# A hybrid encoder block on one core: 252 intermediate stores move from SyncE's DMA queue to GpSimd's, and none of them is held back any more

## The chip, the core and the metric

The kernel runs on one core of one Trainium2 chip. A core has a matrix engine (TensorE, PE in the profile; its weight loads are listed as PEld), three engines for elementwise work (VectorE or DVE, ScalarE or ACT, GpSimd or POOL) and SyncE (SP), which in this kernel only issues DMA transfers. ScalarE and GpSimd issue DMA transfers too, so there are three queues: "SPq", "ACTq" and "POOLq" in the profile. An engine issues in the order of its program: an instruction that waits for a semaphore holds everything behind it on that engine.

The metric is the time on the device in microseconds (us), as the median of several executions. One further execution is taken with the hardware profiler; "the profile" and "the trace" mean that one.

## The reference, cut to what matters

The block works on x of 2048 frames by 1024 channels in float32, one layer deep.

```python
h = rmsnorm(x, norm_mix_pre)
u_pool, u_glu, g_a, g_b = split(h @ w_in)          # 512 | 1024 | 1024 | 1024 columns
# branch A: per group of 128 channels the trailing mean over 2, 4, 8 or 16 frames
#           minus the frame itself, a 128x128 map, a scale, then @ w_pool_out (512 -> 1024)
# branch B: a * sigmoid(gate), causal depthwise convolution of width 31 over 512 channels,
#           LayerNorm over the channels, silu, then @ w_conv_out (512 -> 1024)
merged = sigmoid(g_a) * branch_a + sigmoid(g_b) * branch_b
x = x + rmsnorm(merged @ w_o, norm_mix_post)
h = rmsnorm(x, norm_mlp_pre)
f = square(relu(h @ w_up)) @ w_down                # 1024 -> 4096 -> 1024
out = x + rmsnorm(f, norm_mlp_post)
```

## The kernel before, in words

*Layout.* Channels lie on the 128 partitions and frames run along the free axis. The 2048 frames are two blocks (b = 0, 1) of TB = 1024, each of two halves (t = 0, 1) of T = 512. The usual tile is 128 x 1024 in float32, 512 KB: a cell (256 channels by 512 frames), or a part of a weight.

*Matrix products.* Each float32 operand is split into a high part, rounded by a ScalarE copy (L225 for weights), and a low part, source minus high part, by a VectorE subtraction (`sub`, L121). `matmuls` (L268) adds three products: high by high, high by low, low by high. One call is 12 matmuls of 128 x 128 by 128 x 512 for four blocks of the contraction in the full form of `product`, which calls it for both halves of the output: 24 matmuls.

*Seven products for eight.* The class `Octet` computes a 2 x 2 scheme of cells by weight parts with seven block products, so weights and cells are needed not only as they are but as sums and differences. `weight_parts` makes those of a weight: `get` loads a raw part into one of four `wr` buffers, `minus` makes a sum in one of two `ws` buffers, `split_w` writes the high part into one of three `wh` buffers and the low part into one of three `wl` buffers. For block b = 0 the parts that will be needed again are stored in DRAM (`save`; the names are kept<-wl for low parts and kept<-ws for sums). For b = 1 they are loaded instead of made (wl<-kept, and the sums into `wr`). `load_w` does the same for the weights of the branches and of the output projection, `Plain` for the first part of the input projection.

*Stages.* TensorE's order is: input projection of b = 0 (glu, pool, gates ga and gb), branch A of b = 0, input projection of b = 1, branch B and merge of b = 0, output projection of b = 0, branch A of b = 1 (about 800 us), up projection of the MLP for b = 0, then branch B, merge and output projection of b = 1, the up projection for b = 1, and the down projection of both blocks until the end (the last 600 us), in which VectorE and ScalarE also form the cells of each step (`token_cells`). The final norm and the output stores come last. Convolution (L937), LayerNorm and pooling run on VectorE behind the products, spread over them by "lanes" that release a few steps after each product; those of b = 0 run while TensorE is at the input projection of b = 1.

*What passes through DRAM.* SBUF doesn't hold all intermediates, so these go to DRAM and come back: GLU results (vd, two halves per result) and pool inputs (ud), convolution and LayerNorm results (yd, stored from `y` after the convolution and from `tr` after the mean is taken off), results after the activation (zd) and after the pool map (mxd), sigmoids of the gates (sad, sbd), results of branch A (mad), x after the mixer (x1d), MLP activations and their sums (fd), sums of the down weights (wsum). The buffers from which they are stored (`tr` has 9, `big` 28, `y` one, `fo` five) come free when the store has landed.

*Queues.* Three helpers issue transfers: `load` on SyncE (L127), `aside` on GpSimd (L131) and `store` on ScalarE (L135). Despite its name, `load` carries all loads from DRAM but eight (x for the first output projection comes by `aside`) and most stores. `aside` also has the stores of the halos at the start, the first four low parts of `Plain`, and x1d of the first output projection. `store` has sad, sbd and the plain fd results. The final output goes by `load`, but two cells of it that GpSimd adds onto the output (L1878).

*The deferring lists.* Stores of kept weight parts are not issued where the part is made. `save` and `load_w` append them to the list `later`. After each product `flush` is called: it issues what is in `due` by `load`, last entry first, and moves `later` into `due`. So a part made before one product is issued as a store only after the next call.

*What sets the order.* The program is traced in the order of the Python code, and a planner then orders each engine's instructions by priorities: a region under `tc.high_priority(offset=n)` counts as n places earlier (260 for weights, `AHEAD`; 1500 for `URGENT`), and `mark`, `ordered` and `behind` add order without waiting. Instructions for one engine, DMA issues among them, come in one sequence. The planner also decides which buffer of a pool a tile takes.

Of the kernel before, what the change touches and what calls it, by code (L numbers as in the profile page):

```python
# [67 lines left out]
def block_kernel(  # L68
# [165 lines left out]
    def load_w(src, key):  # L234
        with tc.high_priority(offset=ahead[0]):
            raw = mk(p_wr, "wr")
            load(raw, src)
            known = kept.get((key, "low"))
            w = split_w(raw) if known is None else None
            if key is None:  # L240
                return w
        if w is None:
            with tc.high_priority(offset=260):
                w = split_w(raw, low=known)
        if known is None:
            kept[key, "low"] = dram("kept")
            later.append((kept[key, "low"], f32(w[1])))
        return w

    kept, later, due = {}, [], []  # L250

    def flush():

        while due:
            load(*due.pop())
        due.extend(later)
        later.clear()

# [46 lines left out]
    def weight_parts(src, key, b, keep, raw):  # L305
# [34 lines left out]
        def save(i, what, tile):  # L340
            kept[key, i, what] = dram("kept")
            later.append((kept[key, i, what], f32(tile)))

# [82 lines left out]
    class Octet:  # L426
# [18 lines left out]
        def run(self, i, then, bg):  # L445
            w, cells = self.w.pop(i, None) or self.weight(i), self.parts.need(i)
            if then is not None:
                self.parts.need(then)
            acc = {1: "x", 2: "z", 6: "x", 5: "y", 7: "x", 3: "y", 4: "x"}[i]
            if i in (1, 2, 5):  # L450
                self.ps[acc] = psum(self.lab)
            ps = self.ps[acc]
            product(ps, w, cells, start=i in (1, 2, 5), stop=i in (2, 3, 4))
            flush()
            if i == 1:
                self.s1 = self.held(ps)
                if self.s2 is not None:
                    self.sink(0, 0, self.s2, self.s1)
            elif i == 2 and self.s1 is None:
                self.s2 = self.held(ps)  # L460
            elif i == 2:
                self.sink(0, 0, ps, self.s1)
            elif i == 6:
                self.s6 = self.held(ps)
            elif i == 5:
                self.s5 = self.held(ps)
            elif i == 7:
                self.sink(1, 1, ps, self.s5)
            elif i == 3:
                self.sink(0, 1, ps, self.s6)  # L470
            else:
                self.sink(1, 0, ps, None)
            bg()
# [3 lines left out]
    class Plain:  # L477
# [30 lines left out]
        def run(self, job, then, bg):  # L508
# [7 lines left out]
            product(self.ps, w, cells, start=k == 0, stop=k == 1)  # L516
            flush()
            bg()
# [346 lines left out]
    def glu(b, parts):  # L865
        def one(u):
            sg = {}

            def sink(m, t, ps, s):
# [6 lines left out]
                if t in sg and (t, 1) in sg:  # L876
                    o = sg[t]
                    mul(o, o, sg[t, 1])
                    for i in (0, 1):
                        at = TAPS - 1 + b * TB + t * T  # L880
                        load(vd[2 * u + i][:, at : at + T], o[:, i * T : (i + 1) * T])

# [6 lines left out]
    def pool_in(b, parts):  # L889
        def sink(m, t, ps, s):  # L890
            o = block_out(ps, s)
            if o is ps:
                o = tr()
                mark(nc.scalar.copy(o, ps))
            for i in (0, 1):
                at = HALO + b * TB + t * T
                load(ud[2 * m + i][:, at : at + T], o[:, i * T : (i + 1) * T])

# [16 lines left out]
    def conv_steps(b, groups, ahead=True):  # L915
# [8 lines left out]
        for c in groups:  # L924
# [22 lines left out]
            else:  # L947
                add(sums[b], sums[b], acc)
            load(yd[b, c, 0], acc)
            yield  # L950

    def norm_steps(b, lag):
# [21 lines left out]
        for c in range(CC):  # L974
            if c + 2 < CC:
                prefetch(c + 2)
            sub(y[c], y[c], mu)
            load(yd[b, c, 0], y[c])
            sq = ss if c == 0 else tr()
# [16 lines left out]
        for c in range(CC + 1):  # L996
# [11 lines left out]
            if c:  # L1008
                mul(y[c - 1], y[c - 1], sg[c - 1])
                load(zd[b, c - 1, 0], y[c - 1])  # L1010
            yield 1
# [9 lines left out]
    def pool_steps(b, alone):  # L1021
# [9 lines left out]
        for g in range(CC):  # L1031
# [29 lines left out]
            yield  # L1061
            load(mxd[b, g, 0], o)
            yield
# [34 lines left out]
    def branch_a(b, mixed, bg):  # L1098
# [8 lines left out]
        for (c, t), sg in ahead_by_one(keys, gate_of, 2):  # L1107
# [5 lines left out]
            mark(i)  # L1113
            flush()
            with tc.high_priority(offset=URGENT):
                mark(mul(sg, ps, sg))
            load(mad[b, c, t], sg)
            bg()

    def merge(b, bg, made=none):  # L1120
# [11 lines left out]
        for (c, t), (sg, ma) in ahead_by_one(keys, gate_of, 1 + b):  # L1132
# [5 lines left out]
            mark(i)  # L1138
            flush()
            mark(mul(sg, ps, sg))  # L1140
# [12 lines left out]
    def out_proj(b, merged, halves, bg, made, early=none):  # L1153
# [13 lines left out]
        for ts in halves:  # L1167
            sq = {t: Squares(TR) for t in ts}
            for c in range(CPS):
                ws = [load_w(w_o[c % 2, 2 * (c // 2) + i], ("wo", c, i)) for i in (0, 1)]  # L1170
                for t in ts:
# [8 lines left out]
                    mark(i_mm)  # L1180
                    flush()
                    o[c, t] = mk(*BIG)
# [108 lines left out]
    def out_proj_2(b, cells, made):  # L1291
# [6 lines left out]
        def make(c, t):  # L1298
            mul(two(o[c, t]), two(o[c, t]), per_token(rbs[t]))
            add(x[c, t], x[c, t], o[c, t])  # L1300
            load(x1d[b, c, t], x[c, t])
            gained(o[c, t], x[c, t], C_MPRE, c)
# [35 lines left out]
        for n, (u, i) in enumerate(WO):  # L1338
# [6 lines left out]
            product(p, w, ops, start=i in (1, 2, 5), stop=i in (2, 4, 3))  # L1345
            flush()
            if i in (1, 6, 7):
# [50 lines left out]
    def mlp_up(b, parts):  # L1398
        def one(u):
# [3 lines left out]
            def sink(m, t, ps, s):  # L1403
# [7 lines left out]

                def keep(i, cell, how=load):
                    fd[b, u, i] = dram("fd")
# [254 lines left out]
    def weight_down(i, s, o):  # L1668
# [6 lines left out]
        def joined(op, p, q):  # L1675
            t = mk(p_ws, "ws")
            op(t, get(p), get(q))
            if i in (5, 6):
                wsum[s, o] = dram("wsum")
                load(wsum[s, o], t)  # L1680
            return t
# [12 lines left out]
    def token_cells(s, i, b, home=TR, hi_home=BIG):  # L1694
# [11 lines left out]
        with tc.high_priority(offset=AHEAD):  # L1706
            cells = []
            for j in (0, 1):
# [4 lines left out]
                if m is not None:  # L1713
# [4 lines left out]
                    if i == 6:  # L1718
# [3 lines left out]
                        fd[b, u, "t4"] = dram("fd")  # L1722
                        load(fd[b, u, "t4"], t4)
                hi = mk(*hi_home, F32R)
# [292 lines left out]
```

## Time and profile before

| | us |
|---|---|
| median of 3 runs | 2190.27 |
| lowest and highest | 2186.27, 2196.49 |
| the profiled execution | 2191.51 |
| its span (first to last instruction) | 2189.7 |
| TensorE busy | 2159.9 (99%) |
| VectorE busy | 1610.3 (74%) |
| ScalarE busy | 1017.6 (46%) |
| GpSimd busy | 18.2 (1%) |

The mean granted clock of TensorE in the profiled execution is 0.995 of full speed. In all, 552.30 MB are moved.

How to read the rows: `L121 DVE` is line 121 of the kernel on VectorE; `wl<-kept` is an operation that writes a tile named wl from one named kept (for a DMA, the transfer from DRAM to the buffer); `x72` is a count. A row of waits names the engine that waited, what it wanted to run, and after the arrow what ended the wait, with total us, number of waits and the longest. A row of the chain gives start, length and what ran; the chain is followed back from the last instruction, to what released each step. In the list of DMA issues, the three numbers with slashes are the shortest, median and longest time in ns that an issue takes on its engine.

### The profile page before, as it was taken

The numbers are of one execution on the slowest core, as the hardware profiler recorded it, in microseconds if no ns is written. First come the engines' busy times: TensorE is split into PE (matmuls) and PEld (weight loads), VectorE is DVE, ScalarE is ACT, GpSimd is POOL, SyncE is SP. The second block draws the span as 40 slices with busy tenths as digits, with TensorE's granted clock in tenths as the row PEclk, the third lists the DMA queues.
The fourth block names the chain that finished last, engine by engine and source line by source line (L and its number), as shares of the span: only waits on it lengthen the run. The fifth ranks groups of instructions, "written<-read, shape, count | busy, mean of one in ns | idle before, by whom it ended". The sixth has DMA issues, their size and how long they took to land.

```text
span 2189.7 us, 24848 instructions
## 1 busy us (share of the span) xinstructions
PE 2159.9 (99%) x9582; PEld 1783.8 (81%) x9582; DVE 1610.3 (74%) x1570; ACT 1017.6 (46%) x1060; POOL 18.2 (1%) x41
## 2 busy tenths in 40 slices
PE   9999999999999999999999999999999999999997
PEld 7888888788878878888888878888888888888886
DVE  8898788998688998987757765756644746546884
ACT  6444454334543535545635775555522423334542
POOL 1000000000000000000000000000000000000000
PEclk9999999999999999999999999999999999999998
DMA  7688897678997787435787585644877875545782
GB/s 273 239 298 316 322 345 277 228 256 295 334 371 249 254 321 267 179 144 192 278 295 271 214 284 195 225 169 161 315 283 281 309 273 183 203 156 190 273 299 71
DMA packets 153943, 552.30 MB, mean 252 GB/s; under 512 B 17216, under 2 KB 17472, under 8 KB 153792
## 3 DMA queue, kind: packets, MB, share of 16 engines
q1 hardware_dynamic: 137728, 492.94, 63.3%
q10 hardware_dynamic: 12672, 46.14, 5.4%
q0 software_dynamic: 3424, 11.63, 1.6%
q8 instruction: 75, 1.23, 0.2%
q14 instruction: 44, 0.36, 0.0%
HBM read 366.00 MB, written 185.69 MB: 252 GB/s over the span
## 4 chain that ended last, share of the span: by engine, by line
PE 91%; DVE 4%; DMA 2%; issue 1%; ACT 1%; SPq 0%; DVEq 0%; ACTq 0%
PE up L268 26%; PE down L268 22%; PE wo L268 7%; PE ga L268 7%; PE glu L268 6%; PE gb L268 6%; PE rb L268 5%; PE B L268 4%; PE A L268 4%; PE pool L268 3%; DMA wl<-kept 1%; DVE y L937 1%; PE rb L563 1%; DVE big L121 1%; DMA wr<-w_in 1%
## 5 line engine op out<-in xcount | busy, mean ns | idle before, releaser
L268 PE MATMUL up<-big,wh 128*128 128x512 f32 x1792 | 480.9, 390 | 2.4 <-DVE big L121 1.6
L268 PEld LDWEIGHTS up<-big,wh 128*128 128x128 f32 x1792 | 335.7, 188 | 74.1 <-DVE big L121 2.7
L225 ACT CAST wh<-wr 128x1024 fp32r<-128x1024 f32 x199 | 209.0, 1052 | 391.3 <-PE up L268 79.3
L937 DVE SCALAR_TENSOR_TENSOR y<-v,cst,y 128x1024 f32<-128x1024 f32 x240 | 307.6, 1282 | 2.8
L268 PE MATMUL down<-big,wh 128*128 128x512 f32 x768 | 287.4, 389 | 0.0
L268 PE MATMUL up<-big,wl 128*128 128x512 f32 x896 | 276.0, 389 | 0.0
L225 ACT CAST wh<-ws 128x1024 fp32r<-128x1024 f32 x126 | 132.4, 1052 | 264.1 <-PE up L268 67.5
L268 PE MATMUL down<-tr,wh 128*128 128x512 f32 x648 | 252.1, 389 | 0.0
L268 PE MATMUL down<-big,wl 128*128 128x512 f32 x696 | 214.3, 389 | 0.0
L121 DVE TENSOR_TENSOR tr<-tr,big 128x1024 fp32r<-128x1024 f32 x100 | 120.7, 1223 | 117.3 <-ACT big L1725 115.1
L121 DVE TENSOR_TENSOR wl<-ws,wh 128x1024 fp32r<-128x1024 f32 x118 | 144.1, 1222 | 81.1 <-ACT wh L225 80.9
L268 PEld LDWEIGHTS up<-big,wl 128*128 128x128 f32 x896 | 168.1, 188 | 34.9
L121 DVE TENSOR_TENSOR wl<-wr,wh 128x1024 fp32r<-128x1024 f32 x122 | 148.7, 1220 | 55.3 <-ACT wh L225 54.5
L1725 ACT CAST big<-tr 128x1024 fp32r<-128x1024 f32 x98 | 101.2, 1050 | 165.9 <-DMA tr<-fd 137.0
L268 PEld LDWEIGHTS down<-big,wh 128*128 128x128 f32 x768 | 144.2, 188 | 29.8
L268 PEld LDWEIGHTS down<-big,wl 128*128 128x128 f32 x696 | 130.6, 188 | 27.2
L268 PEld LDWEIGHTS down<-tr,wh 128*128 128x128 f32 x648 | 121.6, 188 | 25.2
L268 PE MATMUL wo<-big,wh 128*128 128x512 f32 x480 | 128.7, 390 | 0.0
L268 PE MATMUL glu<-big,wh 128*128 128x512 f32 x464 | 125.0, 391 | 2.0 <-ACT wh L225 1.4
L268 PE MATMUL gb<-big,wh 128*128 128x512 f32 x448 | 120.0, 390 | 0.0
L268 PE MATMUL ga<-big,wh 128*128 128x512 f32 x448 | 120.0, 390 | 0.0
L268 PEld LDWEIGHTS wo<-big,wh 128*128 128x128 f32 x480 | 89.9, 188 | 18.5
(204 smaller groups left out, 3269.1 us busy)
## 6 DMA issues: line engine op xcount, KB each, us to landing
tr<-fd SPq DMA_DIRECT2D x110, 512.0 KB, 4.8
wr<-w_down SPq DMA_DIRECT2D x90, 512.0 KB, 5.8
wl<-kept SPq DMA_DIRECT2D x85, 512.0 KB, 4.6
kept<-wl SPq DMA_DIRECT2D x72, 512.0 KB, 5.9
wr<-w_up SPq DMA_DIRECT2D x64, 512.0 KB, 4.4
wr<-w_in SPq DMA_DIRECT2D x60, 512.0 KB, 5.3
fd<-tr ACTq DMA_DIRECT2D x54, 512.0 KB, 3.4
fd<-tr SPq DMA_DIRECT2D x46, 512.0 KB, 3.0
```

Source lines behind the costliest of these rows:

```text
L121: return nc.vector.tensor_tensor(o, a, b, op=ALU.subtract)
L225: nc.scalar.copy(hi[:, :n], src[:, :n])
L268: i = nc.tensor.matmul(ps, w[wp][:, (at + k) * P : (at + k + 1) * P], rhs[k][xp], start=start and n == 0, stop=stop and n == len(order) - ...
L563: nc.tensor.matmul(st[:, at + g : at + g + 1], ss[:, g * P : (g + 1) * P], inv_n, start=start is None or (start and g == 0), stop=stop, sk ...
L937: nc.vector.scalar_tensor_tensor(acc, v[:, k : k + TB], wk, acc, op0=ALU.mult, op1=ALU.add)
L1725: nc.scalar.copy(hi, t)
```

## The change

`kept` stays, `later`, `due`, `flush` and all calls of `flush` go. `save` and `load_w` issue the store of a weight part at once, by `aside`, that is on GpSimd's queue, at the place in the program where the part is made. All other intermediate stores that were issued by `load` on SyncE's queue are issued by `aside` too. In numbers of transfers:

| store | count | KB each |
|---|---|---|
| kept<-wl, kept<-ws | 72, 24 | 512 |
| fd<-tr, fd<-fo | 46, 6 | 512 |
| mad, x1d (second projection), wsum | 16, 8, 16 | 512 |
| yd<-y, yd<-tr, zd, mxd | 8, 8, 8, 8 | 512 |
| vd, ud (halves) | 16, 16 | 256 |

Together they are 252. Loads keep SyncE's queue, and the stores on ScalarE's queue, the final output stores and the transfers that GpSimd had already stay where they are. In the order of the changed program, TensorE's sequence differs at 18 places, all of them small products for statistics. VectorE's differs at about 154 places and ScalarE's at about 85, most of them shifts by a few places. On GpSimd, the second four of the eight x loads of the first projection come behind stores of branch A.

```diff
 def load_w(src, key):
...
         if known is None:
             kept[key, "low"] = dram("kept")
-            later.append((kept[key, "low"], f32(w[1])))
+            aside(kept[key, "low"], f32(w[1]))
...
-    kept, later, due = {}, [], []
-
-    def flush():
-
-        while due:
-            load(*due.pop())
-        due.extend(later)
-        later.clear()
+    kept = {}
...
         def save(i, what, tile):
             kept[key, i, what] = dram("kept")
-            later.append((kept[key, i, what], f32(tile)))
+            aside(kept[key, i, what], f32(tile))
...
             product(ps, w, cells, start=i in (1, 2, 5), stop=i in (2, 3, 4))
-            flush()
...
-                        load(vd[2 * u + i][:, at : at + T], o[:, i * T : (i + 1) * T])
+                        aside(vd[2 * u + i][:, at : at + T], o[:, i * T : (i + 1) * T])
...
-                load(ud[2 * m + i][:, at : at + T], o[:, i * T : (i + 1) * T])
+                aside(ud[2 * m + i][:, at : at + T], o[:, i * T : (i + 1) * T])
...
-            load(yd[b, c, 0], acc)
+            aside(yd[b, c, 0], acc)
...
-            load(yd[b, c, 0], y[c])
+            aside(yd[b, c, 0], y[c])
...
-                load(zd[b, c - 1, 0], y[c - 1])
+                aside(zd[b, c - 1, 0], y[c - 1])
...
-            load(mxd[b, g, 0], o)
+            aside(mxd[b, g, 0], o)
...
-            load(mad[b, c, t], sg)
+            aside(mad[b, c, t], sg)
...
-            load(x1d[b, c, t], x[c, t])
+            aside(x1d[b, c, t], x[c, t])
...
-                def keep(i, cell, how=load):
+                def keep(i, cell, how=aside):
...
-                load(wsum[s, o], t)
+                aside(wsum[s, o], t)
...
-                        load(fd[b, u, "t4"], t4)
+                        aside(fd[b, u, "t4"], t4)
```

More of the change, by code (lines that the diff above doesn't have):

```diff
@@ L516, in run @@
             product(self.ps, w, cells, start=k == 0, stop=k == 1)
-            flush()
             bg()
@@ L1113, in branch_a @@
             mark(i)
-            flush()
             with tc.high_priority(offset=URGENT):
                 mark(mul(sg, ps, sg))
-            load(mad[b, c, t], sg)
+            aside(mad[b, c, t], sg)
             bg()
@@ L1138, in merge @@
             mark(i)
-            flush()
             mark(mul(sg, ps, sg))
@@ L1180, in out_proj @@
                     mark(i_mm)
-                    flush()
                     o[c, t] = mk(*BIG)
@@ L1345, in out_proj_2 @@
             product(p, w, ops, start=i in (1, 2, 5), stop=i in (2, 4, 3))
-            flush()
             if i in (1, 6, 7):
```

## The prediction, made before the changed kernel was run

> **What bounds the kernel now.** I read the engines' busy time first, then the table of stages, then what ended TensorE's idle time, and last SyncE's queue.
>
> ```profile
> PE 2159.9 (99%) x9582; PEld 1783.8 (81%) x9582; DVE 1610.3 (74%) x1570; ACT 1017.6 (46%) x1060; POOL 18.2 (1%) x41
> ...
> HBM read 366.00 MB, written 185.69 MB: 252 GB/s over the span
> ```
>
> TensorE (PE) is busy in 2159.9 of 2189.7 us; GpSimd (POOL) does next to nothing. So a change of queues can win only what TensorE still loses. By stage (columns: length, then busy time of PE, PEld, DVE, ACT and POOL, the granted TensorE clock, the DMA share and GB/s):
>
> ```profile
> 360.00:412.00 52.00, 47.84 (x197) 38.65 (x196) 47.15 (x41) 19.14 (x19) 0.00 (x0) 0.93 0.53 178
> 575.00:615.00 40.00, 38.78 (x170) 31.49 (x169) 25.52 (x21) 23.50 (x22) 0.00 (x0) 1.00 0.92 324
> 755.00:788.00 33.00, 30.56 (x133) 24.57 (x131) 29.05 (x36) 13.39 (x15) 2.70 (x5) 0.95 0.85 316
> 788.00:846.00 58.00, 58.00 (x260) 48.12 (x259) 55.52 (x49) 29.42 (x32) 2.13 (x4) 1.00 0.82 308
> 846.00:876.00 30.00, 29.54 (x130) 24.09 (x130) 24.45 (x22) 16.87 (x17) 0.00 (x0) 1.00 0.70 242
> 1225.00:1300.00 75.00, 73.22 (x332) 59.76 (x331) 61.35 (x70) 58.42 (x68) 0.00 (x0) 1.00 0.74 259
> 1300.00:2090.00 790.00, 790.00 (x3510) 654.61 (x3508) 464.73 (x442) 338.73 (x346) 0.00 (x0) 1.00 0.65 230
> ```
>
> Idle TensorE between opening and end: 52.00 - 47.84 = 4.16, 40.00 - 38.78 = 1.22, 33.00 - 30.56 = 2.44, 30.00 - 29.54 = 0.46, 75.00 - 73.22 = 1.78; together 10.06 us. Two of these stages also ran at a lower clock: 0.07 x 52 = 3.64 and 0.05 x 33 = 1.65 us of lost work. So 15.35 us is all that the middle can give. The other 2189.7 - 2159.9 - 10.06 = 19.7 us of idle TensorE lie in the opening and at the end, outside the change: the first loads and the final output stores stay where they are.
>
> What ended TensorE's idle time (us in total, times, longest):
>
> ```profile
> PE pool L268 <- DVE tr L118: 2.7, 1, 2.7
> ...
> PE gb L268 <- DMA wl<-kept: 1.2, 2, 0.7
> ```
>
> A transfer ended 1.2 us of it. The longest wait of all, 2.7 us, was for VectorE (DVE). Does a store stand behind VectorE? For the largest loss, 360 to 412, the chain of waits answers (start, length, what):
>
> ```profile
> 362.09 1.06 ACT wh L225
> ...
> 363.17 5.42 DMA wr<-w_in
> ```
>
> The load of the weight goes out at 363.17, right after ScalarE's cast at 362.09 has freed its buffer. The load waits for a buffer, not for a store. I leave that loss as it is.
>
> **The change part by part.** SyncE's queue waits long for VectorE:
>
> ```profile
> SPq L127 <- DVE wl L121: 391.1, 100, 14.8
> SPq L127 <- DVE ws L121: 252.2, 67, 13.9
> ```
>
> These waits mix stores (data not made yet) with loads (buffer not free yet), so they bound the loads' possible lead, not TensorE's gain. Removed from the queue are 252 stores, by the profile's list of DMA issues (its longest entry, kept<-wl x72, and its shortest, fd<-fo x6, stand below): 96 of weight parts, 52 of MLP results, 40 of cells and weight sums (mad, x1d, wsum), 32 halves for convolution and pooling, 32 of convolution, LayerNorm and pool results. Nothing is copied or computed less or more.
>
> *Issue.* Each store needs a sequencer's time on both sides:
>
> ```profile
> L127 SPq DMA_DIRECT2D kept<-wl x72: 319/374/937, 31.1 to 877.1; - x72
> ...
> L131 POOL DMA_DIRECT2D x1d<-big x8: 531/534/536, 742.8 to 807.3; - x8
> ```
>
> SyncE gets back about 252 x 0.374 = 94 us, GpSimd takes on 252 x 0.534 = 135 us, 6% of the span, in an engine 99% idle: zero on the path. If that cover went (a burst), a store would go out 0.53 us later per store ahead of it, and a buffer of its source would come free as much later.
>
> *Landing.* The same kinds of store on both queues (size, median us to landing):
>
> ```profile
> kept<-wl SPq DMA_DIRECT2D x72, 512.0 KB, 5.9
> ...
> x1d<-big POOLq DMA_DIRECT2D x8, 512.0 KB, 4.6
> x1d<-big SPq DMA_DIRECT2D x8, 512.0 KB, 6.8
> fd<-fo SPq DMA_DIRECT2D x6, 512.0 KB, 4.2
> kept<-wl POOLq DMA_DIRECT2D x4, 512.0 KB, 6.4
> ```
>
> No difference in either direction: one pair is 2.2 us shorter from GpSimd, the other 0.5 us longer. I take zero. The same 124 MB are moved as before (220 stores of 512 KB, 32 of 256 KB), so the engines have no more to do.
>
> *Loads that stood behind a store.* Between 575 and 615 SyncE's queue shows it:
>
> ```profile
> 602.05 0.32 SPq L127 DMA_DIRECT2D zd<-tr  x1
> 604.40 0.33 SPq L127 DMA_DIRECT2D wr<-w_co  x1
> 604.83 0.39 SPq L127 DMA_DIRECT2D wl<-kept  x1
> ```
>
> The store zd<-tr at 602.05 waits for VectorE's product, two loads are behind it, and the second is the weight part that TensorE waits for. Without the store, both can go out earlier, unless w_co still waits for ScalarE's cast. Between nothing and the whole 1.22 us of this stage I take the whole: both loads followed within 604.83 - 602.05 = 2.78 us of the store, so it was the store that held them.
>
> *Stores that held a buffer.* The deferring lists go, so a weight part is stored when it is made:
>
> ```profile
> DVE ws L121 <- DMA kept<-ws: 10.7, 4, 4.3
> ```
>
> Of these waits the chain shows one:
>
> ```profile
> 861.74 1.15 DVE ws L121
> ...
> 863.79 8.22 DMA kept<-ws
> ```
>
> VectorE stood 10.7 us in four waits until a stored sum released its buffer. In the chain, the sum is made until 862.9, stored from 863.79 and landed at 872.0, in the stage that lost 0.46 us. On its own queue the store need not go behind the loads issued before it, so I take 0.46 us as won, all of that stage. The other waits I price at zero: most of TensorE's remaining losses end at VectorE work, not at these.
>
> *Eight loads that now stand behind stores.* GpSimd's queue already has the eight loads of x for the first projection. The second four come behind a result of branch A in the new order. Before:
>
> ```profile
> 780.66 0.54 POOL L131 DMA_DIRECT2D big<-xt  x1
> ```
>
> ```profile
> 781.73 5.76 SPq L127 DMA_DIRECT2D mad<-tr  x2
> ```
>
> That store of branch A went out from SyncE at 781.73, so the loads start about 782.3, 1.6 us later, and VectorE's additions may be that much later. Cost between 0 and 1.6 us. I take 0: from 788 to 846, where these additions run, TensorE has no gap at all.
>
> *Order of work.* The planner keeps TensorE's order but for a few small statistics products, and moves some VectorE and ScalarE operations by a few places, mostly at the two changes from a gate to a branch or the output projection. A VectorE operation on a whole tile takes 1.15 us (the row of 861.74). Two places at two such changes are 4 x 1.15 = 4.6 us, for or against. I take 0, the middle.
>
> Sum: -1.22 - 0.46 = -1.7 us. The profiled execution took 2191.51 us (span 2189.7), so 2189.8; the median of the three runs, 2190.27, lies 1.24 below it, which gives 2188.6 us.
>
> One rule supports a still smaller effect. The Trainium skill, "DMA: Bandwidth & Descriptors", section "Issuing engines are not separate DMA queues", says that DMAs from several engines end on the same 16 engines, and that more issuers save only the sequencer's time. By it the sum would be 0 and the time 2190.3 us. The rows of landing agree with it; the zd row above is the kind of sequencer's time that it allows.
>
> **The rivals.**
>
> *A, nothing moves.* The change promises "at once", but the sum made until 862.9 left at 863.79 in the old queue already, and the wait for data is only moved into another queue. Then nothing changes: 2190.3 us. For it: TensorE is busy for 58.00 of 58.00 and 790.00 of 790.00 us in two stages. Against it: the zd row.
>
> *B, the loads run ahead.* With no store in front, loads come early enough that VectorE never falls behind and all 15.35 us vanish: 2191.51 - 15.35 - 1.24 = 2174.9 us. For it: 391.1 and 252.2 us of waiting in the queue. Against it: 363.17, where a buffer, not a store, decides; VectorE is also busy for 47.15 of 52 us there.
>
> *C, stores overtake loads (slower).* In one queue a store waits its turn behind loads; from another queue it shares the engines with them. The place is 575 to 615, where the engines are 92% busy and TensorE takes weight parts straight from DMA:
>
> ```profile
> L127 SPq DMA_DIRECT2D wl<-kept x7: 319/387/628, 575.4 to 609.0; - x7
> ...
> DMA to landing us min/median/max: 3.6/6.3/9.4
> ```
>
> ```profile
> 98.08 5.44 PE glu L268 x24
> ```
>
> A 512 KB store is 524288 / 252000 = 2.08 us of all engines at the mean rate of 252 GB/s. A load has some two products, 10.9 us, between buffer and use (the row of 98.08: one product, 24 matmuls, in 5.44 us; two are 10.88). It decides when a landing of 9.4 passes 10.9, that is 1.5 us more. If all seven loads lose 2.08 us to TensorE: 14.6 us, 2203.2 us. For it: 9.4 us of landing. Against it: TensorE waited only 1.2 us for all transfers.
>
> The Trainium skill, "DMA: Bandwidth & Descriptors", section "Queues, rings and completion order", states that an engine takes its queues in turn, packet by packet. That is what C supposes, and no row before the change shows two such busy queues beside each other.
>
> **How the numbers follow.** A measurement of this kernel, with runs from 2186.27 to 2196.49, can tell about 0.5%, 11 us. Forecast (a few us either side of 2188.6, my own range 2183 to 2195): 0.43. A: 0.20. B or most of it: 0.12. C, or another new wait of that size in the tight VectorE stages: 0.25. Forecast and A are both within 0.5%: same 0.63, faster 0.12, slower 0.25. The range runs from near B (2176) to beyond C (2205), and leaves out about half of B and a quarter or more of C.
>
> **What would show it.** Right: stores on q0 and some 124 MB gone from q1; the wait for zd gone from SyncE's queue; TensorE's wait for wl<-kept near 0, VectorE's for kept<-ws well below 10.7 us, the loss at 360 to 412 still there. Wrong, towards B: the lower clock at 360 to 412 gone. Wrong, towards C: PE waits for wl<-kept or wr loads of over 5 us, landings in q1 above 10 us, or VectorE operations beside GpSimd's issues clearly longer than before.

## The result: 1% slower, and the profile after

| | before | after |
|---|---|---|
| median, us | 2190.27 | 2211.60 |
| lowest and highest of 5 runs | 2184.01, 2196.49 | 2209.69, 2216.44 |
| profiled execution, its span | 2191.51, 2189.7 | 2209.96, 2208.2 |

The ratio after to before is 1.0101, with a 95% interval of 1.0089 to 1.0113: 21.3 us more by the medians. That lies outside the range of the prediction (2176 to 2205).

The engines' busy time and the queues, from the page of the changed kernel:

```profile
PE 2165.8 (98%) x9582; PEld 1784.8 (81%) x9582; DVE 1607.7 (73%) x1570; ACT 1016.6 (46%) x1060; POOL 153.2 (7%) x293
...
q1 hardware_dynamic: 101440, 369.19, 47.6%
q0 software_dynamic: 37664, 135.38, 15.6%
...
HBM read 366.00 MB, written 185.69 MB: 250 GB/s over the span
```

No engine has more work but GpSimd, by 153.2 - 18.2 = 135.0 us, as forecast. The stores have moved to q0 (135.38 MB). Most of the time went into waits: between 60 and 1330 us TensorE is idle for 24.4 us in the changed kernel's trace and for 10.2 in the one before. The stages of the changed kernel show where (columns as in the prediction's table; the places lie later by what was lost before them):

```profile
60.00:130.00 70.00, 70.00 (x311) 57.96 (x310) 63.42 (x56) 31.32 (x31) 16.17 (x30) 1.00 0.71 257
130.00:165.00 35.00, 32.24 (x138) 25.90 (x137) 30.53 (x28) 10.84 (x12) 5.95 (x11) 0.95 0.65 248
...
290.00:370.00 80.00, 76.70 (x335) 62.20 (x334) 71.65 (x63) 37.09 (x44) 8.03 (x15) 1.00 0.88 331
370.00:420.00 50.00, 46.71 (x206) 38.00 (x205) 47.09 (x41) 19.31 (x20) 3.77 (x7) 1.00 0.55 193
...
590.00:640.00 50.00, 47.36 (x208) 38.53 (x207) 37.29 (x31) 27.38 (x27) 3.21 (x6) 1.00 0.90 338
...
720.00:760.00 40.00, 36.89 (x164) 30.25 (x163) 34.97 (x40) 14.32 (x18) 1.08 (x2) 0.96 0.73 280
760.00:830.00 70.00, 66.44 (x293) 54.26 (x292) 63.03 (x66) 31.75 (x40) 11.80 (x22) 0.98 0.81 303
830.00:900.00 70.00, 66.53 (x290) 53.64 (x289) 58.86 (x51) 37.89 (x39) 10.69 (x20) 1.00 0.75 276
...
1320.00:2100.00 780.00, 780.00 (x3465) 646.25 (x3464) 454.26 (x434) 330.57 (x337) 25.65 (x48) 1.00 0.64 231
```

There is no single hole. TensorE loses about 3 us in each of seven places, all in the first 900 us, where VectorE has the most to do (one of them lost as much before: 4.16 us from 360 to 412); from 1320 to 2100 nothing is lost. The waits of TensorE say the same:

```profile
PE gb L261 <- DVE tr L118: 3.5, 2, 2.6
PE wo L261 <- DMA wl<-kept: 3.1, 1, 3.1
PE up L261 <- DVE big L121: 3.1, 4, 1.1
PE rb L554 <- DVE tr L118: 2.6, 1, 2.6
PE A L261 <- DVE tr L124: 2.2, 1, 2.2
```

Most of them end at VectorE; the 3.1 us for a weight part (wl<-kept) don't, and the section on the prediction comes back to them. So the main question is what made VectorE late. It isn't slower at its work: its busy time is 1607.7 us against 1610.3.

A view that helps more than totals sets the two traces against each other product by product. TensorE runs the same products with weights (8760 matmuls, those for statistics and the pool map left out) in the same order, so the start of the n-th matmul in one trace less its start in the other is the lag at that point, and a step in the lag is a loss at a place. This table is worked out from the records of the traces; the first columns are the matmul's number and its start in the kernel before, the others the lag in us of the changed kernel and of experiments that are described below.

```
  n   before  after    e1    e2    e3    e4    e5    e6   e13
 456   119.7    1.0   0.2   0.8  -0.3  -0.5  -0.4   1.1  -0.5
 552   141.4    5.8   0.3   3.2   3.7  -0.1   0.7   2.5  -0.5
1200   296.8    7.2   0.5   9.3  10.9   0.1   0.9   2.7   1.2
1392   340.3   10.5   0.5  11.8  11.0   0.1   2.6   3.0   6.1
1632   402.3    6.7  -0.6   9.6  10.0  -2.3   0.9  -0.8   4.4
2760   669.5    8.7  -1.9  14.2  10.4   2.1   2.1   0.4   7.5
3144   758.4   14.2   3.2  14.2  10.7   2.1   6.2   2.8   9.7
4680  1117.9   18.8   2.9  22.1  16.0   6.3  11.1   0.9  17.9
8759  2166.6   18.5   2.4  23.8  15.7   7.7  10.7   0.5  18.2
```

### The profile page after: what moved, and what is told of

The parts are those of the page before. It is cut to its first block, busy times and chain, and to the rows that moved or that the text cites. A ratio compares the mean times of both kernels' runs of the same rounds, so it can differ in the third digit from the quotient of the medians.

```text
span 2208.2 us, 25052 instructions
## 1 busy us (share of the span) xinstructions
PE 2165.8 (98%) x9582; PEld 1784.8 (81%) x9582; DVE 1607.7 (73%) x1570; ACT 1016.6 (46%) x1060; POOL 153.2 (7%) x293
## 3 DMA queue, kind: packets, MB, share of 16 engines
q0 software_dynamic: 37664, 135.38, 15.6%
## 4 chain that ended last, share of the span: by engine, by line
PE 74%; issue 14%; DVE 4%; DMA 4%; POOL 2%; ACT 1%; SPq 0%; POOLq 0%; DVEq 0%; ACTq 0%
PE up L261 24%; PE down L261 23%; PE glu L261 6%; PE rb L261 5%; PE B L261 4%; PE wo L261 4%; PE gb L261 3%; PE ga L261 2%; DMA big<-xt 2%; DVE y L928 1%; POOL kept L131 1%; PE A L261 1%; PE pool L261 1%; DVE big L121 1%; PE rb L554 1%
## 5 line engine op out<-in xcount | busy, mean ns | idle before, releaser
L928 DVE SCALAR_TENSOR_TENSOR y<-v,cst,y 128x1024 f32<-128x1024 f32 x240 | 307.6, 1282 | 2.6
```

Source lines behind the costliest of these rows:

```text
L928: nc.vector.scalar_tensor_tensor(acc, v[:, k : k + TB], wk, acc, op0=ALU.mult, op1=ALU.add)
```

## The experiments

Two theories stood at the start. *Q, the queue*: stores on a second queue run beside the loads, so loads land later. In the changed trace they do: over the 689 loads of SyncE's queue the mean from issue to landing went from 5.75 to 6.28 us, and loads of more than 10 us from 21 to 67. *O, the order*: the planner, which no longer sees the stores in SyncE's queue, orders loads, VectorE and ScalarE differently, and that order is worse.

### The order by itself, in both directions

The first two kernels separate the theories. A list with the order of one kernel's instructions on TensorE, VectorE, ScalarE and of SyncE's loads is imposed on the other kernel by links that order without waiting; the moved stores are left free:

```diff
+    for engine, packed in ORDERS.items():
+        steps = np.frombuffer(zlib.decompress(base64.b85decode(packed)), "<i2")
+        mine = [i for i in nc.cur_bb.bb.instructions if ... i.name not in free]
+        line = [mine[k] for k in np.cumsum(steps.astype(int))]
+        for p, q in zip(line, line[1:]):
+            tc.add_manual_dep(q, p.name, NOSYNC, reason="one order")
```

*e1*, the changed kernel in the order of before:

> The changed kernel, its 252 stores on GpSimd's queue at once, but TensorE's, VectorE's and ScalarE's instructions and SyncE's loads are held to the order that they have in the kernel before. Theory O (the planner's other order of loads and vector work costs the 21 us): about 2190 us, as before. Theory Q (stores on a second queue share the 16 DMA engines with loads, which land later): about 2211 us, as the changed kernel, with a mean landing of the loads near its 6.3 us and not the 5.75 us of before. Half and half would give about 2200.

*e2*, the kernel before in the order of the changed one:

> The mirror image: the kernel before, stores on SyncE's queue and weight parts deferred, but loads, TensorE, VectorE and ScalarE held to the order of the changed kernel. Theory O: about 2211 us. Theory Q: about 2190 us, landings near 5.75 us. The stores may stand less well between loads that were not ordered for them, so a few us above either are possible.

Measured: e1 2196.77 us, ratio 1.0040 (1.0024 to 1.0055); e2 2213.03 us, ratio 1.0112 (1.0097 to 1.0128). So the other order alone, with every store where it was on SyncE's queue, costs as much as the whole change. With the old order 2211.60 - 2196.77 = 14.8 of 21.3 us come back, and 6.5 stay. Theory O holds for most of it. In the lag table e1 stays within 1 us of the kernel before at every point listed up to 402 us, where the changed kernel is up to 10.5 behind.

### Which stores bring the order about

*e3* moves only the 96 stores of weight parts:

```diff
-            later.append((kept[key, "low"], f32(w[1])))
+            aside(kept[key, "low"], f32(w[1]))
...
-            later.append((kept[key, i, what], f32(tile)))
+            aside(kept[key, i, what], f32(tile))
```

> Only the 96 stores of weight parts go to GpSimd's queue, at once; the other 156 stay on SyncE's. They are 50 of the 124 MB that moved. Theory Q, by bytes: 0.4 x 21 = 8.5 us slower than before, about 2199. Theory O: TensorE's order stays that of before, VectorE's and the loads' order moves less than in the changed kernel, so 2190 to 2195.

*e4* moves only the other 156; the deferring lists stay:

```diff
-            load(mad[b, c, t], sg)
+            aside(mad[b, c, t], sg)
...
-                def keep(i, cell, how=load):
+                def keep(i, cell, how=aside):
...
```

> Only the other 156 stores (cells, convolution, LayerNorm, MLP results, wsum) go to GpSimd's queue; weight parts stay deferred on SyncE's. Theory Q, by bytes: 0.6 x 21 = 13 us slower than before, about 2203. Theory O: nearly the whole change of order comes with these stores, so about 2207 to 2211.

Measured: e3 2203.81 us, ratio 1.0069 (1.0055 to 1.0083), e4 2194.47 us, ratio 1.0026 (1.0013 to 1.0039). That is the reverse of both expectations: 50 MB (96 x 512 KB) cost 13.5 us, 73 MB cost 4.2. How much of the order moves doesn't tell the price either. Counted by names in the traces, 23 of VectorE's 1570 operations and 8 of the 689 loads stand out of the order of before in e3, 69 and 41 in e4 (75 and 45 in the changed kernel). What counts is which operations move.

*e7* and *e8* are e4 and e3 with everything held to the order of before. Stores that stay on SyncE's queue are left out of the list by a helper:

```diff
+    def put(o, src):
+        i = load(o, src)
+        free.add(i.ins.name)
+        return i
```

> Only the 156 stores that are not weight parts go to GpSimd's queue, all else in the order of before. With the order out of the way only the second queue is left. If it costs by bytes (theory Q), 0.6 x 6.5 = 3.9 us over before: about 2194. If a weight part's store is what meets the loads, about 2190.

> Only the 96 stores of weight parts go to GpSimd's queue, all else in the order of before. Theory Q by bytes: 0.4 x 6.5 = 2.6 us over before, about 2193. The same 96 stores with their own order took 2203.8: the difference is what the order costs.

Measured: e7 2188.53 us, ratio 0.9998 (0.9988 to 1.0007); e8 2191.40 us, ratio 1.0014 (1.0002 to 1.0026). Without the change of order, the other stores cost nothing on GpSimd's queue, and the weight parts about 2 us, at the edge of what the runs can tell. The same weight parts with their own order (e3) cost 12.4 us more than e8.

### Loads or vector work

*e5* holds only SyncE's loads, *e6* only TensorE, VectorE and ScalarE to the order of before:

```diff
     for engine, packed in ORDERS.items():
+        if engine not in ("SP",):     # e6: ("PE", "DVE", "Activation")
+            continue
```

> The changed kernel with only SyncE's loads held to the order of the kernel before; TensorE, VectorE and ScalarE are planned as they come. Of the 21.3 us, the whole order accounts for 14.8 (2211.6 against 2196.8 with the order of before). Theory L (loads that stand behind other loads whose buffer isn't free): about 2197. Theory V (VectorE takes weight sums ahead of other work): about 2210.

> The mirror image: TensorE, VectorE and ScalarE held to the order of before, SyncE's loads planned as they come, which leaves them nearly in the order of the changed kernel. Theory L: about 2210. Theory V: about 2197.

Measured: e5 2203.14 us, ratio 1.0063 (1.0049 to 1.0077); e6 2191.77 us, ratio 1.0013 (1.0002 to 1.0024). Holding the engines brings back 2211.60 - 2191.77 = 19.8 us. Holding the loads alone brings back 2211.60 - 2203.14 = 8.5, a result between the two theories; so theory L, by which only the loads' order mattered, is not borne out, and neither is V for e5. The two runs don't separate loads from vector work cleanly, because the planner plans anew what isn't held. In e6's trace 15 of the 689 loads stand out of the changed kernel's order and 42 out of that of before, but at the two places read below they stand as in the kernel before. So e6 shows that the engines' order is enough to bring the time back (more than with the loads held too, 2196.77 in e1), not that the loads' order costs nothing.

e6 also ends theory Q as the main cause. Its loads land as late as those of the changed kernel, and it takes 20 us less:

```
                      before  after    e2     e6    e7    e8
mean landing, us        5.75   6.28   5.93   6.30  5.97  5.96
loads over 10 us          21     67     34     66    36    39
time, us             2190.27 2211.60 2213.03 2191.77 2188.53 2191.40
```

The mean is over the 689 loads of SyncE's queue in each trace. e2 is the other half of the proof: its landings are nearer to those of before than to those of the changed kernel, and its time is the longest of these.

*e10* and *e11* split e6 by engine, with ("DVE",) and ("Activation",) in that line.

> The changed kernel with VectorE's instructions alone held to the order of before. With TensorE, VectorE and ScalarE held it took 2191.8. If VectorE's order is what costs: 2190 to 2195. If it needs ScalarE's too: 2203 or more.

> The changed kernel with ScalarE's instructions alone held to the order of before. If VectorE's order is what costs, this takes about as long as the changed kernel, 2207 to 2212. If ScalarE's order is what costs, 2190 to 2195.

Measured: e10 2198.20 us, ratio 1.0039 (1.0024 to 1.0054); e11 2205.22 us, ratio 1.0067 (1.0051 to 1.0083). Holding VectorE's order brings back 13.4 us and holding ScalarE's 6.4. Both help, VectorE's more, but these aren't separate shares: with VectorE held, the planner leaves 22 of ScalarE's operations out of the order of before instead of 37, and with ScalarE held, 60 of VectorE's instead of 75. That the two add up to the 19.8 of e6 proves nothing.

### One place in full

Between 119.7 and 141.4 us the changed kernel falls 4.8 us behind. In its trace VectorE and SyncE's queue do this (start, length, engine, what; in brackets the idle time before and what ended it):

```profile
121.69 1.22 DVE L121 TENSOR_TENSOR ws<-wr,ws 128x1024 f32<-128x1024 f32 x1
122.94 1.23 DVE L121 TENSOR_TENSOR ws<-wr,wr 128x1024 f32<-128x1024 f32 x1
...
137.96 1.23 DVE L118 TENSOR_TENSOR tr<-tr,tr 128x1024 f32<-128x1024 f32 x1 [4.47 <-ACT tr L683]
```

```profile
122.94 2.13 SPq L127 DMA_DIRECT2D wr<-w_in  x3
125.11 1.94 SPq L127 DMA_DIRECT2D tr<-xt  x2
```

and the chain of waits:

```profile
125.11 11.65 DMA tr<-xt
...
136.87 1.07 ACT tr L683
137.94 0.03 issue
137.96 1.23 DVE tr L118
```

A weight sum (122.94) was moved ahead. On SyncE's queue, three weight loads go out as this sum and the one before it free their inputs, and the two loads of x for the statistics now stand behind them. The first lands 11.65 us later at 136.8. VectorE has no other work ahead of the sum over x in its order, so it stands still for 4.47 us, and TensorE waits soon after:

```profile
128.79 1.52 PE L261 MATMUL pool<-big,wh 128*128 128x512 f32 x6
...
138.88 1.92 PE L261 MATMUL pool<-big,wh 128*128 128x512 f32 x6 [1.77 <-ACT tr L432]
...
147.25 1.67 PE L261 MATMUL ga<-big,wh 128*128 128x512 f32 x6 [0.99 <-ACT wh L225]
```

The first wait ends with a copy on ScalarE, whose trace shows why: ScalarE waits 7.67 us for the same load of x, until 136.87, and the copy (tr L432, at 137.84) stands behind the operation on x. The two waits are 1.77 + 0.99 = 2.8 of the 4.8 us. Most of the rest is a lower clock right after the first: the granted clock is 0.65 from 138.8 to 143.2 us (1.00 in the whole stretch of the kernel before), that is 0.35 x 4.4 = 1.5 us of lost work, and six matmuls take 1.92 us instead of 1.52.

In the kernel before, the same weight sum came later and the x load earlier. The rows of VectorE and of SyncE's queue there:

```profile
127.93 1.22 DVE L121 TENSOR_TENSOR ws<-wr,wr 128x1024 f32<-128x1024 f32 x1
...
130.26 1.22 DVE L118 TENSOR_TENSOR tr<-tr,tr 128x1024 f32<-128x1024 f32 x1
```

```profile
120.88 0.33 SPq L127 DMA_DIRECT2D wr<-w_in  x1
121.26 0.45 SPq L127 DMA_DIRECT2D kept<-ws  x1
121.76 0.42 SPq L127 DMA_DIRECT2D tr<-xt  x1
```

*e13* restores this place alone (the order list is cut to a stretch on VectorE, ScalarE and the loads):

```diff
+    PART = {'DVE': (100, 200), 'Activation': (60, 105), 'SP': (28, 47)}
...
+        line = line[slice(*PART[engine])]
```

> The changed kernel with the order of before at one place only, about 100 to 160 us: one weight sum, its low part and its high part on VectorE and ScalarE, and two x loads that stand ahead of two weight loads on SyncE's queue again. In the changed kernel VectorE waited 4.5 us there for x, and TensorE fell 5.0 us behind between 120 and 153 us. If that wait is the cause and the loss isn't given back later: 2206 to 2207. If the places make up for each other: 2210 to 2212.

Measured: 2208.43 us, ratio 1.0082 (1.0068 to 1.0095). The row of VectorE's sum over x in e13:

```profile
130.41 1.23 DVE L125 TENSOR_TENSOR tr<-tr,tr 128x1024 f32<-128x1024 f32 x1 [0.42 <-ACT tr L692]
```

The wait of 4.47 us is 0.42, and the lag at matmul 552 goes from 5.8 to -0.5. So it is shown that the order at this place makes the loss there. But the time falls by only 2211.60 - 2208.43 = 3.2 us, which lies between the two expectations and at the edge of the noise: in the lag table e13 is 6 us ahead of the changed kernel at 141 us, 4.4 at 340 and 0.9 at 1118. What one place gains, the later places take in large part.

e13 restores the sum and the loads at once. Two other traces tell them apart. In e5 the weight sum still stands ahead (at 120.84), but the x loads go out before two of the three weight loads: the first lands 8.2 us after its issue, VectorE waits 1.50 us for it, and the lag at matmul 552 is 0.7. So most of the wait comes from the order of the loads and not from the sum's own place on VectorE. In e2 the order is that of the changed kernel and the stores are on SyncE's queue: the x loads land after 8.4 and 9.4 us instead of 11.7 and 12.7, VectorE waits 1.05 and 1.72 us, and the lag grows by 2.4 us instead of 4.8. At this place, then, the loss is twice as large with the later landings that theory Q names.

The second large step, from 296.8 to 340.3, looks alike, but no run restores it alone. In the changed kernel's trace:

```profile
299.97 1.33 SPq L127 DMA_DIRECT2D big<-xt  x3
...
308.98 2.28 SPq L127 DMA_DIRECT2D tr<-sad  x3
```

```profile
321.47 1.23 DVE L124 TENSOR_TENSOR tr<-A,tr 128x1024 f32<-128x1024 f32 x1 [8.02 <-DMA tr<-sad]
```

The gates of branch A (sad) are loaded behind x for the next stage, and VectorE waits 8.02 us for the first; before, the three loads went out at 297.50 and it waited 1.99:

```profile
297.50 1.89 SPq L127 DMA_DIRECT2D tr<-sad  x3
```

```profile
306.90 1.23 DVE L124 TENSOR_TENSOR tr<-A,tr 128x1024 f32<-128x1024 f32 x1 [1.99 <-DMA tr<-sad]
```

Such a wait of VectorE isn't TensorE's loss in full. Of the 8.02 us TensorE stood still for 2.2 (the row "PE A" above). In e6 VectorE waits 5.78 us at this operation, and the lag grows by only 0.3 us:

```profile
314.30 1.23 DVE L132 TENSOR_TENSOR tr<-A,tr 128x1024 f32<-128x1024 f32 x1 [5.78 <-DMA tr<-sad]
```

*e14* and *e15* restore the first part, up to about 350 us, and the rest:

```diff
+    PART = {'DVE': (0, 330), 'Activation': (0, 210), 'SP': (0, 110)}
...
+    PART = {'DVE': (330, None), 'Activation': (210, None), 'SP': (110, None), 'PE': (0, None)}
```

> The changed kernel with the order of before in its first part only (VectorE, ScalarE and loads up to branch A of the first block, about 350 us). TensorE's lag there was 10.5 of 18.5 us in the profiled executions. If the losses add up by places: 2211.6 - 10 = about 2202.

> The complement: the changed kernel with the order of before from branch A of the first block on, its own order ahead of that. If the losses add up: 8 us of lag lie in this part, of which the run with the whole order of before kept some 3 to 6 as the queue's own, so 2211.6 - 3 to - 6 = 2206 to 2209.

Measured: e14 2204.77 us, ratio 1.0069 (1.0055 to 1.0083), that is 6.8 us back instead of 10; e15 2205.59 us, ratio 1.0068 (1.0055 to 1.0080), 6.0 back. The sum, 12.8, is near the 14.8 of e1: the loss is spread over the kernel and doesn't sit at one place. (e14's trace is of an execution of 2217.07 us, so its places aren't read.)

### The queue or the "at once"

*e9* takes only the deferring lists away and stores weight parts at once on SyncE's queue:

```diff
-            later.append((kept[key, i, what], f32(tile)))
+            load(kept[key, i, what], f32(tile))
...
-            flush()
```

> The kernel before with one half of the change: the deferring lists go and weight parts are stored at once, but all stores stay on SyncE's queue. If taking the stores off SyncE's queue is what makes the planner order VectorE's work worse, this stays within a few us of before: 2188 to 2194. If storing at once does it, 2200 or more.

*e17* is the other half: all 252 stores on GpSimd's queue, and the deferring lists stay:

```diff
         while due:
-            load(*due.pop())
+            aside(*due.pop())
```

> The other half of the change alone: all 252 stores go to GpSimd's queue, but weight parts are still held back by the deferring lists. In the order that the planner makes of it, TensorE, VectorE, ScalarE and the loads stand as in the changed kernel. If the order is what costs, 2209 to 2214 us, and the deferral is worth nothing on either queue. If storing at once on GpSimd is what costs, 2190 to 2200.

Measured: e9 2191.78 us, ratio 1.0003 (0.9992 to 1.0014); e17 2218.94 us, ratio 1.0140 (1.0116 to 1.0163). Storing at once costs and wins nothing on SyncE's queue, and holding back doesn't help on GpSimd's. It is the queue that brings the other order about: in e9's trace 16 of VectorE's 1570 operations and 6 of the 689 loads stand out of the order of before, and in e17's all of VectorE, ScalarE and the loads stand as in the changed kernel. That e17 takes 7 us more than the changed kernel, though only two stores in it stand in another order, I can't explain: the mean landing is 6.36 us, and its four runs spread from 2213.70 to 2225.33.

### What is left when the order is right

In e1, with the order of before, 6.5 us remain. In the lag table they arise between 669.5 and 758.4 us (from -1.9 to 3.2). In its trace VectorE waits longer for the one buffer of the convolution, whose store now stands among the weight parts' on GpSimd's queue:

```profile
687.35 0.82 DVE L934 TENSOR_SCALAR y<-v,cst 128x1024 f32<-128x1024 f32 x1 [6.57 <-DMA yd<-y]
```

Before, that wait was 3.07 us:

```profile
685.79 0.81 DVE L933 TENSOR_SCALAR y<-v,cst 128x1024 f32<-128x1024 f32 x1 [3.07 <-DMA yd<-y]
```

*e12* puts these eight stores back on SyncE's queue, in e1:

```diff
-            aside(yd[b, c, 0], acc)
+            put(yd[b, c, 0], acc)     # load, left out of the order list
```

> The first experiment (252 stores on GpSimd's queue, all else in the order of before, 2196.8) with only the eight stores of convolution results put back on SyncE's queue, where they stood. The convolution has one buffer, and in that experiment VectorE waited 6.6 us for such a store to land, 3.5 more than before. If that wait is the residue of 6.5 us: 2191 to 2194. If the residue is a mean effect of 124 MB on a second queue: 2196 to 2197.

Measured: 2195.13 us, ratio 1.0019 (1.0007 to 1.0031). VectorE's wait is 3.1 us again in its trace, and 1.6 us are won, but the interval overlaps that of e1. This is unclear: the wait is at most a part of the residue. Another part may be a wait of TensorE for a weight part (wl<-kept): 1.87 us at 718.56 in e1, 0.31 in e12, none there before. It is read with the x loads in the next section.

*e16* was meant to beat both kernels. It is e4 with the list for ("PE", "DVE", "Activation") alone:

> A candidate to beat both: the 156 stores that aren't weight parts go to GpSimd's queue, VectorE, ScalarE and TensorE keep the order of before, and SyncE's loads are planned anew. With the loads held too it took 2188.5, and on the changed kernel free loads were 5 us better than held ones (2191.8 against 2196.8). If that gain carries over: 2184 to 2186, else 2188 to 2191.

Measured: 2190.53 us, ratio 1.0000 (0.9991 to 1.0009). It equals the kernel before. None of the kernels is measurably faster than before; e7 (0.9998) and e16 are equal to it.

## Why the prediction was wrong, point by point

- **What bounds the kernel: right.** TensorE is busy in 98% and nothing else became the bound. That at most 15.35 us were to be won stays untested; nothing was won. 5.3 us of it were to come from a lower clock, and the low clock at 360 to 412 is indeed gone (a sign towards B in the prediction), though the kernel got slower. It only moved: the clock records show two drops to 0.5 between 60 and 1330 us before (6.8 us long from 394.4, 3.4 from 773.3) and three after (3.4 us each, from 140.1, 730.6 and 785.2), half of 10.2 us and so 5.1 us of lost work in both.
- **Issue: right.** GpSimd's busy time grew by 135.0 us, and e7 shows 156 of the stores there at no cost; how far the residue of e1 hangs on this queue is open.
- **Landing: right for the sum, not at every place.** The prediction took zero. Loads land 0.5 us later in the mean, and 67 instead of 21 take more than 10 us. e6 has the same landings at 2191.77 us; but at the first place above the loss was twice as large with them as without (e2).
- **Loads that stood behind a store: not borne out.** In the changed kernel the stage that answers to 575 to 615 lost 50.00 - 47.36 = 2.64 us instead of 1.22. The term was also misread. The zd store was issued at 602.05 and took 0.32 us; the load behind it went out only at 604.40, when a cast on ScalarE had freed its buffer, as the chain of the kernel before says:

```profile
603.35 1.04 ACT wh L225
...
604.40 0.33 SPq L127
```

  So the store didn't hold the two loads, and the 2.78 us between them don't show that it did. The stage lost 0.37 us in e7, which moves the zd stores in the order of before, but nothing in e9, which leaves them on SyncE's queue; the times of both equal that of before (ratios 0.9998 and 1.0003).
- **Stores that held a buffer: the wait shrank, the time didn't.** VectorE's waits for kept<-ws fell from 10.7 to 5.9 us:

```profile
DVE ws L121 <- DMA kept<-ws: 5.9, 2, 4.4
```

- **Eight loads behind stores: the wrong four.** The prediction looked at the second four. The first four moved most: from 667.81 to 716.22, behind stores of weight parts, where they go out together with the weights:

```profile
715.55 0.53 POOL L131 DMA_DIRECT2D kept<-wl  x1 [6.90 <-DVE wl L121]
716.22 2.43 POOL L131 DMA_DIRECT2D big<-xt  x4
```

  They bring the longest wait of TensorE in the changed kernel. These loads take 9.5 to 15.3 us to land (3.7 to 6.7 before), and the weight part issued among them, at 719.62, takes 9.8 us where the one of before took 5.2; TensorE waits 3.1 us for it (PE wo <- DMA wl<-kept). e1 has the same burst at 705.42 and a wait of 1.87, e8 at 701.37 and none, and in e2, where the loads went out at 682.04, there is none. No run moves these four loads alone, so their price by itself is not shown. The second four went out at 798.77 instead of 780.66, some 4 us later than TensorE's lag there (14.2), where the prediction had 1.6.
- **Order of work: this is the step that failed.** "Two places at two such changes are 4 x 1.15 = 4.6 us, for or against. I take 0, the middle." The runs show 14.8 us for the whole order (e1) and 19.8 with the engines' order alone held (e6). The mistake is in the price of a shift. I priced it at the operation's own length, 1.15 us, and counted only VectorE and ScalarE. But the loads on SyncE's queue change their order too (45 of 689), and what a shift costs is the wait of the first operation whose data is late: at the first place 4.47 us on VectorE and 7.67 on ScalarE, for x loads behind weight loads, and 4.8 us more lag on TensorE; at the second 8.02 us on VectorE and 3.3 more lag. And I counted two changes of stage, where TensorE loses about 3 us in each of seven places.
- **The rivals.** C had the right sign, but its mechanism (stores that delay loads in the shared engines) isn't the main cause: e6 has the delay without the loss, and e2 has the loss with little of the delay. It has a share at the first place and in the wait for the weight part at 729.50; no wait of TensorE for wl<-kept or wr reached the 5 us that were to be its sign, though landings above 10 us, its other sign, grew from 21 to 67. Its 2203.2 us came nearer to the result only by chance. A and B are out.
- **The chances.** Slower had 0.25, on "C, or another new wait of that size in the tight VectorE stages". The second half of that names the kind of thing that came, but without a mechanism, a place or a price. That the planner's order could fall out worse was seen only as a term of 4.6 us, taken as 0, and not as a rival. The queue's waits, up to 14.8 us in one, were a reason for a wider bound.
- **The Trainium skill.** "DMA: Bandwidth & Descriptors", section "Issuing engines are not separate DMA queues": e7 (0.9998) and e8 (1.0014) agree with it: with the order held, moving stores to another issuing engine won nothing. By it the prediction had 2190.3 us; that a planner answers with another order lies outside of it.

What stays open: why the planner moves just these operations (that it sees SyncE's queue emptier is an argument, not shown), the residue of e1, the 7 us of e17, and whether the planner's choice of buffers, which can change with the order, has a share: no run separates the two.

## What to carry to other kernels

Where a planner orders the engines, moving a DMA from one queue to another is also a change of the program's order: hold the old order to measure the queue alone, and compare orders before believing that "only stores moved". Price a moved operation or load by what it will stand in front of, not by its own length, and look at the order of the loads too. In a stage where the vector engine had little slack and fed the matrix engine, two loads that stood behind three others cost TensorE 4.8 us here, four times the length of the operation that had moved.

## What was not expected of the hardware

With the order held, 73 MB of stores on GpSimd's queue changed the time by no more than 0.12% either way (e7), though the mean landing of loads grew from 5.75 to 5.97 us. With all 124 MB there, 6.5 us remain (e1), so it isn't shown that a second queue is free. VectorE's operations keep their length beside GpSimd's 252 more DMA issues: the convolution step has a mean of 1282 ns in both kernels (before, then after):

```profile
L937 DVE SCALAR_TENSOR_TENSOR y<-v,cst,y 128x1024 f32<-128x1024 f32 x240 | 307.6, 1282 | 2.8
L928 DVE SCALAR_TENSOR_TENSOR y<-v,cst,y 128x1024 f32<-128x1024 f32 x240 | 307.6, 1282 | 2.6
```
